# Second feed-forward product of a hybrid encoder block: block products of eight in place of plain products

## The chip, the cores and the metric

One Trainium2 chip, one of its cores. The metric is the device time of one execution of the whole program in microseconds (us). Engines are called PE (TensorE, matmuls), PEld (its weight loads), DVE (VectorE), ACT (ScalarE), POOL (GpSimd) and SP (SyncE, which here only starts DMA transfers).

## What is computed

The block takes x (1024 tokens of 1024 channels, float32) through a state-space branch, a sparse attention branch, a merge and a feed-forward part. Only the last part matters here:

```
h2 = rmsnorm(x, norm2_g)
g, up = split(h2 @ w_ffn_in, [2816])
x = x + (silu(g) * up) @ w_ffn_out
out = rmsnorm(x, norm_f_g)
```

`h2 @ w_ffn_in` is the first product (1024 channels in, 5632 out) and `(silu(g) * up) @ w_ffn_out` the second (2816 in, which is 22 tiles of 128, and 1024 out, which is 8 tiles of 128). All tensors lie transposed: channels on the 128 partitions, tokens along the free dimension, in halves H0 and H1 of 512.

## The kernel before, in words

**Precision.** Every operand is split into a high and a low part (`whi`, `wlo` for weights): ACT casts it to the matmul's format (`S.copy`, line 190, or line 88 in `load_w`), DVE subtracts the cast from the original (line 191, or 89). One product of a 128x128 weight tile with 512 tokens is then three matmuls: high by high, high by low, low by high.

**First product** (`ffn_pair`, lines 804 to 857, called 22 times at line 1040). One call makes one tile of `g` and one of `up` for all tokens. It treats them as a 2x2 block product and forms it, as Winograd's form of Strassen's scheme does, from seven block products in place of eight. A block product is 4 contraction tiles x 3 = 12 matmuls of 512 columns, so a call has 84. Four sums of weights (`s1` to `s4`) are formed on POOL (lines 811 to 814). The seven activation operands (`b11, t1, t2, b21, t3, b22, t4`) were formed earlier; each lies split in one of seven slots of 16 KB per partition (`mb0, mb1, ma0, ma1, c0, c1, c2`, given out by `slot`). Each block product has a PSUM bank of its own, taken in turn from `px` and `pg` (four banks each); DVE (line 836) and ACT (line 841) add the seven results to `gate` and `hid`. Then POOL multiplies `gate` by the row norm (line 853), ACT takes Silu (854), POOL multiplies again (855), DVE multiplies `hid` by it (856), and `hid` goes to a DRAM scratch `hscr` (857).

**Second product** (lines 1066 to 1095). The 22 contraction tiles are taken in stages of 8, 6, 4 and, as the tail, 4. `acts_in` (1041) reads `hscr` tile by tile, 512 KB each (line 1050), into a staging buffer (`hin`) and splits it into slots that are free again. Within a stage each of the 8 output tiles takes its weights by `load_w` and runs `fout` (859) on both halves: n contraction tiles x 3 matmuls into one bank, then one copy by ACT or one add by DVE into `x2[m]`. In the second stage the residual comes back from `x2scr` (`xin`, line 1086) and POOL adds it (1087).

**Tail** (lines 1114 to 1123). The last tiles run in token chunks of 512, 256 and 256. After each chunk the sum of squares is closed, the row norm is formed (`rstd_bcast`), and `finish` scales and writes the output.

**Staging buffers.** Two rotating buffers each lie under the names `eh` and `el` of pool `ep` (bufs=2, 4 KB per partition each). In the first product `gate` is an `eh` tile and `hid` an `el` tile; later `xin` takes `eh`, and the `hin` of the later stages take `el`. The first stage's `hin` use six buffers: two called `raw` and the four in which the weights `ra` and `rw` of the first product had been.

**Order of work.** The program is written engine by engine, and a scheduler in the compiler fixes the order of each engine's instructions beforehand; each engine and SP's queue then runs its list in order. A tile that finds no free buffer of its name waits until one is released.

Of the kernel before, what the change touches and what calls it, by code (L numbers as in the profile page):

```python
# [8 lines left out]
F32 = mybir.dt.float32  # L9
# [11 lines left out]
KT = 8  # L21
# [9 lines left out]
FT = FFN // P  # L31

# [8 lines left out]
AIN = 3  # L41
# [4 lines left out]
RAWT = None  # L46
# [11 lines left out]
def block_kernel(ctx, tc, xT, gv, wk, wfo, rope, s5s, s5b, s5c, ldt, dsk, cst, cm, out):  # L58
# [119 lines left out]
    hscr = dram.tile([FT, P, L], F32, name="hscr")  # L178
# [625 lines left out]
    def ffn_pair(j, B, ft, sm, first, hook=None):  # L804
        ra, rw = [wp.tile([P, KT, P], F32, tag="raw", name="raw") if first or t == RAWT else
                  ft.tile([P, KT, P], F32, tag=t, name=t, bufs=2) for t in ("ra", "rw")]
        SP.dma_start(out=ra, in_=wk[T_FFN + j])
        SP.dma_start(out=rw, in_=wk[T_FFN + FT + j])
        a11, a12, a21, a22 = ra[:, :4], ra[:, 4:], rw[:, :4], rw[:, 4:]
# [5 lines left out]
        state = {"n": 0}  # L815

        def mul(a, b):
            n = state["n"]
            if n % 2 == 0:
                state["w"] = (wp.tile([P, KT, P], F32R, tag="whi", name="whi"),  # L820
                              wp.tile([P, KT, P], F32R, tag="wlo", name="wlo"))
            state["n"] += 1
            hi, lo = [t[:, 4 * (n % 2):4 * (n % 2) + 4] for t in state["w"]]
            split(hi, lo, a)
            ps = (px, pg)[n % 2].tile([P, 512], F32, tag="xg"[n % 2], name="pm")
            for k in range(4):
                PE.matmul(ps, hi[:, k], b[:, k], start=(k == 0), stop=False)  # L827
                PE.matmul(ps, hi[:, k], b[:, 4 + k], start=False, stop=False)  # L828
                PE.matmul(ps, lo[:, k], b[:, k], start=False, stop=(k == 3))  # L829
            return ps  # L830

        def T(tag):
            return ft.tile([P, 512], F32, tag=tag, name=tag, bufs=2)

        def add(o, a, b):
            V.tensor_tensor(o, a, b, op=OP.add)  # L836
            return o
        gate = ep.tile([P, L], F32, tag="eh", name="gate")
        hid = ep.tile([P, L], F32, tag="el", name="hid")
        m1 = T("m1")  # L840
        S.copy(m1, mul(a11, B["b11"]))
        u2 = add(T("u2"), mul(s2, B["t2"]), m1)
        u3 = add(T("u3"), mul(s3, B["t3"]), u2)
        m5 = mul(s1, B["t1"])
        u4 = add(T("u4"), m5, u2)
        add(hid[:, H1], m5, u3)
        add(gate[:, H1], mul(s4, B["b22"]), u4)
        if hook:
            hook()
        add(gate[:, H0], mul(a12, B["b21"]), m1)  # L850
        add(hid[:, H0], mul(a22, B["t4"]), u3)
        for c in (H1, H0):
# [3 lines left out]
            V.tensor_tensor(hid[:, c], hid[:, c], gate[:, c], op=OP.mult)  # L856
        SP.dma_start(out=hscr[j], in_=hid)

    def fout(c, n, ws, acts, m, x2, first=False):
        hi, lo = ws  # L860
        ps = pg.tile([P, 512], F32, tag="g", name="g")[:, :c.stop - c.start]
        for k in range(n):
            PE.matmul(ps, hi[:, k], acts[k][0][:, c], start=(k == 0), stop=False)  # L863
            PE.matmul(ps, hi[:, k], acts[k][1][:, c], start=False, stop=False)  # L864
            PE.matmul(ps, lo[:, k], acts[k][0][:, c], start=False, stop=(k == n - 1))  # L865
        if first:
            S.copy(x2[m][:, c], ps)
        else:
            V.tensor_tensor(x2[m][:, c], ps, x2[m][:, c], op=OP.add)  # L869
# [137 lines left out]
    xg = xgp.tile([P, KT, L], F32, name="xg")  # L1007
    B = {"b22": slot("c0"), "t3": slot("c1"), "t2": slot("c2")}
# [29 lines left out]
    ft = tc.alloc_tile_pool(name="ft", bufs=1)  # L1038
    for j in range(FT):
        ffn_pair(j, B, ft, sm, j == 0, None if j else lambda: rstd_bcast(ep, ss, rb2, H0))  # L1040
    def acts_in(j0, n, keys, stage):
        r = []
        for q in range(n):
            if q % 2 == 0:
                t = slot(keys[q // 2])
            o = 4 * (q % 2)
            hi, lo = hl(t, o, 2), hl(t, o + 2, 2)
            pool, tag = stage[q % len(stage)]
            raw = pool.tile([P, KT, P], F32, tag=tag, name="hin", bufs=2).rearrange("p a b -> p (a b)")
            SP.dma_start(out=raw, in_=hscr[j0 + q])  # L1050
            split(hi, lo, raw)
            r.append((hi, lo))
        return r

    def tail_weights(k0, n, keys, r):
        for m in range(8):
            if m % 4 == 0:
                wt = slot(keys[m // 4])
            hi, lo = [wt[:, 2 * (m % 4) + q].rearrange("p (k d) -> p k d", k=4) for q in range(2)]
            raw = ep.tile([P, KT, P], F32, tag="el", name="raw")[:, :n]  # L1060
            SP.dma_start(out=raw, in_=wfo[m][:, k0:])
            split(hi, lo, raw)
            r.append((hi, lo))
            yield

    plan = ((8, ("mb0", "c2", "c1", "mb1")), (6, ("c0", "ma0", "ma1")), (4, ("mb0", "c2")), (4, ("c1", "mb1")))
    k0 = 0
    nxt = load_w(0, 8, wfo[0][:, :8])
    acts = acts_in(0, 8, plan[0][1], [(wp, "raw"), (ft, "ra"), (ft, "rw")])
    ft.release()  # L1070
    sm.release()
    xr = tc.alloc_tile_pool(name="xr", bufs=1)
    x2 = [xr.tile([P, L], F32, name=f"x2_{m}") for m in range(8)]
    for q, (n, _) in enumerate(plan[:-1]):
        n2, keys2 = plan[q + 1]
        for m in range(8):
            ws = nxt
            if m < 7:
                nxt = load_w(0, n, wfo[m + 1][:, k0:k0 + n])
            elif q < 2:  # L1080
                nxt = load_w(0, n2, wfo[0][:, k0 + n:k0 + n + n2])
            for c in HALVES:
                fout(c, n, ws, acts, m, x2, q == 0)
            if q == 1:
                t = ep.tile([P, L], F32, tag="eh", name="xin")
                SP.dma_start(out=t, in_=x2scr[m])
                G.tensor_tensor(x2[m], x2[m], t, op=OP.add)
            if m == AIN:
                acts2 = acts_in(k0 + n, n2, keys2, [(ep, "el")])
            if q == 2:  # L1090
                if m == 0:
                    wts = []
                    tw = tail_weights(k0 + n, n2, ("c0", "ma0"), wts)
                next(tw)
        acts = acts2
        k0 += n
    n = n2
    nt = [r32(slot("ma1")), r32(slot("mb0"))]
# [16 lines left out]
    for c in (H0, slice(512, 768), slice(768, 1024)):  # L1115
        for m in range(8):
            fout(c, n, wts[m], acts, m, x2)
            add_sq(x2[m][:, c], ss[:, c], m == 0)
            if m == 4 and last:
                finish(last)  # L1120
        rstd_bcast(ep, ss, rb2, c)
        last = c
# [85 lines left out]
```

## Time and profile before

| | us |
|---|---|
| three runs of the kernel | 1956.57 (median), 1956.02, 1960.09 |
| profiled execution, first to last instruction (its span) | 1953.5 |
| median less span, taken as what lies around the profiled span | 3.1 |
| first feed-forward product, from the trace | 1266.2 to 1692 |
| second product, stages of 8, 6 and 4 | 1692 to 1891 |
| tail, norm and output | 1891 to 1953.5 |

No time of its own is recorded for the profiled execution beside its span, so its own time is taken as span plus 3.1, which is the median.

How to read it: times of the trace count from the first instruction. PE's matmuls are pipelined, so a row shows 0.39 us for a matmul whose successor starts 0.23 us later; the pitch from start to start is what counts. "Idle before, releaser" names who ended a wait.

### The profile page before, as it was taken

How to read it: one execution, taken by the hardware profiler on the slowest of the kernel's cores; microseconds unless marked ns; L12 is line 12 of the kernel's file. 1: busy time of each engine (PE TensorE's matmuls, PEld its weight loads, DVE VectorE, ACT ScalarE, POOL GpSimd, SP SyncE). 2: the span in 40 equal slices, each digit the busy share in tenths (PEclk: the TensorE clock that was granted, in tenths of full speed). 3: DMA queues.
4: the chain of work that ended last, by engine and by line, in shares of the span. 5: the costliest groups of instructions: out<-in, count | busy, mean ns of one | idle time of the engine just before them, and what ended most of it. 6: DMA issues, size and time to landing. Idle time of an engine off the chain costs nothing.

```text
span 1953.5 us, 23933 instructions
## 1 busy us (share of the span) xinstructions
PE 1829.1 (94%) x8502; PEld 1510.8 (77%) x8502; DVE 1388.8 (71%) x2253; ACT 851.0 (44%) x1432; POOL 741.9 (38%) x512
## 2 busy tenths in 40 slices
PE   7999999996988888899999899999999999999997
PEld 6888777885766677777887678878888888788886
DVE  7966798779989878966568656786767666812355
ACT  5322245445455776145666744632332323422124
POOL 5168765446765321100000001356656566301303
PEclk9999999997999999999999999999999999999998
DMA  4553443422222332162237455432122221523322
GB/s 171 165 188 115 147 115 112 131 82 63 88 78 84 111 119 86 65 205 82 91 124 237 156 199 188 158 108 92 76 87 85 77 93 69 204 95 95 113 66 87
DMA packets 137447, 229.94 MB, mean 118 GB/s; under 512 B 26608, under 2 KB 78832, under 8 KB 137328
## 3 DMA queue, kind: packets, MB, share of 16 engines
q1 hardware_dynamic: 134704, 225.22, 35.1%
q10 hardware_dynamic: 2624, 3.20, 0.5%
q8 instruction: 67, 1.10, 0.2%
q14 instruction: 52, 0.43, 0.1%
HBM read 158.91 MB, written 66.06 MB: 115 GB/s over the span
## 4 chain that ended last, share of the span: by engine, by line
PE 55%; DVE 20%; ACT 6%; POOL 6%; DMA 6%; issue 5%; SPq 1%; DVEq 0%; ACTq 0%; POOLq 0%
PE pm L829 6%; PE pm L827 6%; PE pm L828 6%; PE g L865 4%; PE g L864 4%; PE g L863 4%; PE g L680 4%; PE g L681 4%; PE g L682 4%; DVE sc L358 2%; ACT junk L622 2%; PE g L208 2%; PE g L209 2%; PE g L207 2%; DVE wlo L89 2%
## 5 line engine op out<-in xcount | busy, mean ns | idle before, releaser
L209 PE MATMUL g<-h_hi,wlo 128*128 128x512 f32 (+1 forms) x704 | 277.2, 394 | 22.1 <-DVE wlo L89 22.1
L207 PE MATMUL g<-h_hi,whi 128*128 128x512 f32 (+1 forms) x704 | 276.8, 394 | 9.5 <-ACT whi L88 7.0
L208 PE MATMUL g<-h_lo,whi 128*128 128x512 f32 (+1 forms) x704 | 277.1, 394 | 2.1 <-DVE h_lo L156 2.1
L89 DVE TENSOR_TENSOR wlo<-raw,whi 128x1024 fp32r<-128x1024 f32 (+2 forms) x117 | 146.7, 1254 | 63.8 <-ACT whi L88 63.6
L209 PEld LDWEIGHTS g<-h_hi,wlo 128*128 128x128 f32 x704 | 135.4, 192 | 51.0 <-DVE wlo L89 25.8
L207 PEld LDWEIGHTS g<-h_hi,whi 128*128 128x128 f32 x704 | 135.4, 192 | 35.2 <-ACT whi L88 7.0
L88 ACT CAST whi<-raw 128x1024 fp32r<-128x1024 f32 (+2 forms) x89 | 88.4, 993 | 160.1 <-PE g L864 79.3
L208 PEld LDWEIGHTS g<-h_lo,whi 128*128 128x128 f32 x704 | 135.1, 192 | 29.2 <-DVE h_lo L156 3.5
L358 DVE SCALAR_TENSOR_TENSOR sc<-r,wq,sc 128x384 f32<-128x384 f32 (+3 forms) x160 | 148.7, 973 | 9.3 <-ACT r L357 8.4
L357 ACT ACTIVATE r<-ips,rqi 128x384 f32<-128x384 f32 (+3 forms) x160 | 93.8, 615 | 86.0 <-PE ips L356 47.0
L622 ACT ACTIVATE junk<-sc,nthr 128x384 bf16<-128x384 f32 (+1 forms) x124 | 96.3, 776 | 68.2 <-DVE nthr L618 66.0
L88 POOL CAST whi<-raw 128x1024 fp32r<-128x1024 f32 x28 | 33.9, 1212 | 220.2 <-PE g L681 105.6
L829 PE MATMUL pm<-c,wlo 128*128 128x512 f32 x264 | 103.7, 393 | 2.3 <-DVE wlo L191 2.3
L827 PE MATMUL pm<-c,whi 128*128 128x512 f32 x264 | 103.2, 391 | 0.0
L828 PE MATMUL pm<-c,whi 128*128 128x512 f32 x264 | 103.2, 391 | 0.0
L853 POOL TENSOR_TENSOR gate<-gate,rb 128x512 f32<-128x512 f32 x44 | 67.8, 1541 | 84.2 <-DVE gate L836 84.2
L1018 POOL TENSOR_TENSOR xg<-xg 128x512 f32<-128x512 f32 x4 | 7.1, 1779 | 240.7 <-ACT xg L791 240.7
L191 DVE TENSOR_TENSOR wlo<-s,whi 128x512 fp32r<-128x512 f32 x88 | 93.7, 1085 | 3.5 <-ACT whi L190 3.5
L856 DVE TENSOR_TENSOR hid<-hid,gate 128x512 f32<-128x512 f32 x44 | 53.1, 1209 | 47.4 <-POOL gate L855 47.4
L355 PE MATMUL ips<-ki,st 128*128 128x384 f32 (+3 forms) x160 | 64.9, 406 | 21.7 <-ACT r L357 17.1
L190 ACT CAST whi<-s 128x512 fp32r<-128x512 f32 x88 | 52.5, 621 | 64.8 <-PE pm L828 60.7
L869 DVE TENSOR_TENSOR x<-g,x 128x512 f32<-128x512 f32 (+1 forms) x56 | 34.1, 611 | 61.1 <-PE g L865 61.0
(388 smaller groups left out, 5278.3 us busy)
## 6 DMA issues: line engine op xcount, KB each, us to landing
raw<-in_wk SPq DMA_DIRECT2D x95, 512.0 KB, 4.2
hscr<-hid SPq DMA_DIRECT2D x22, 512.0 KB, 2.6
hin<-hscr SPq DMA_DIRECT2D x22, 512.0 KB, 3.8
ra<-in_wk SPq DMA_DIRECT2D x21, 512.0 KB, 3.2
rw<-in_wk SPq DMA_DIRECT2D x21, 512.0 KB, 3.2
gscr<-go SPq DMA_DIRECT2D x16, 512.0 KB, 4.9
q<-qscr SPq DMA_DIRECT2D x16, 512.0 KB, 4.9
st<-qiscr SPq DMA_DIRECT2D x16, 384.0 KB, 3.9
```

The source lines that it names most:

```text
L88: (eng or S.copy)(hi[:, :kt], raw[:, :kt])
L89: V.tensor_tensor(lo[:, :kt], raw[:, :kt], r32(hi[:, :kt]), op=OP.subtract)
L191: V.tensor_tensor(lo, src, r32(hi), op=OP.subtract)
L207: PE.matmul(ps, hi[:, k], act[0][:, k, c], start=(k == 0), stop=False)
L208: PE.matmul(ps, hi[:, k], act[1][:, k, c], start=False, stop=False)
L209: PE.matmul(ps, lo[:, k], act[0][:, k, c], start=False, stop=(k == KT - 1))
L357: S.activation(r, ps, AF.Relu, scale=rqi[:, i:i + 1])
L358: V.scalar_tensor_tensor(seg(i)[:, c], r, wq[:, i - 2, h:h + 1], seg(i)[:, c], op0=OP.mult, op1=OP.add)
L622: S.activation(junk2[:, :n], seg(j + 2), AF.Sign, bias=nthr.bitcast(F32)[:, j:j + 1], accum_out=cnt[:, j:j + 1])
L827: PE.matmul(ps, hi[:, k], b[:, k], start=(k == 0), stop=False)
L828: PE.matmul(ps, hi[:, k], b[:, 4 + k], start=False, stop=False)
L829: PE.matmul(ps, lo[:, k], b[:, k], start=False, stop=(k == 3))
```

## The change

**Second product.** 16 of the 22 contraction tiles (`WK = 16`) are taken as two groups (g = 0, 1) of eight. A group is a block product of 4 pairs of contraction tiles with 4 pairs of output tiles (q = 0 to 3), each in seven block products of 12 matmuls (`out_pair`, through the new `winograd`). The last 6 tiles make up the tail, which keeps its three chunks.

**Activations.** The seven operands of a group are formed on DVE in `ffn_pair` from two neighbouring `hid` tiles (four subtractions per two calls) and written to a DRAM scratch `tscr`, 256 KB each, seven per two calls, in place of `hscr`. `refill` brings one operand back into the slot of the same name: two reads of 512 KB into `eh` buffers, each split by ACT and DVE. It is called as soon as the previous user's block product of that name has been written: in the last call of `ffn_pair` for group 0, in the last `out_pair` of group 0 for group 1. In the last `out_pair` of group 1 `tail_fill` loads the tail's operands and weights instead.

**Weights.** `out_raw` loads two output tiles' weights of 8 contraction tiles; POOL forms the four sums, ACT and DVE split seven half tiles, as in the first product.

**Block sums.** In both products four of the seven block products accumulate in one bank (A) one after another, two in a bank B, one alone. ACT or DVE reads the sum out of bank A between two of them. The first product's DVE adds out of PSUM fall from seven to three per call (its last product is multiplied straight out of PSUM), its ACT copies rise from one to three. The order of the seven is now `b11, t1, t2, b21, t3, b22, t4`.

```
+    def winograd(a, B, sm, sink, after=None):
...
+        plan = ((a11, "b11", "A", "m1"), (s1, "t1", "B", "m5"), (s2, "t2", "A", "u2"), (a12, "b21", "D", "d"),
+                (s3, "t3", "A", "u3"), (s4, "b22", "B", "e"), (a22, "t4", "A", "c21"))
...
             for k in range(4):
-                PE.matmul(ps, hi[:, k], b[:, k], start=(k == 0), stop=False)
...
+                PE.matmul(ps, hi[:, k], b[:, k], start=(fresh and k == 0), stop=False, skip_group_check=True)
...
+            sink(stage, ps)
+            if after:
+                after(n, key)
...
+            if stage in ("m1", "m5", "u2"):
+                S.copy({"m1": m1, "m5": m5, "u2": u2}[stage], ps)
...
+            elif stage == "u3":
+                V.tensor_tensor(hid[:, H1], ps, m5, op=OP.add)
...
+            sub(t3, hid[:, H1], h[:, H1])
+            sub(h[:, H1], h[:, H1], h[:, H0])
+            sub(t2, hid[:, H1], h[:, H1])
+            sub(t4, hid[:, H0], t2)
...
+    def refill(key, g):
+
+        t = slot(SLOT[key])
+        for h in range(2):
+            raw = ep.tile([P, L], F32, tag="eh", name="hin")
+            SP.dma_start(out=raw.rearrange("p (k c) -> p k c", k=2),
+                         in_=tscr[ORDER.index(key), 4 * g + 2 * h:4 * g + 2 * h + 2].rearrange("k p c -> p k c"))
+            hi, lo = hl(t, 2 * h, 2), hl(t, 4 + 2 * h, 2)
+            split(hi, lo, raw)
+        return t
...
+    def out_pair(g, q, a, B, sm, x2, after=None):
...
+            if g == 0 and stage in ("m1", "m5", "u2", "c21"):
+                S.copy(x, ps)
+            else:
+                V.tensor_tensor(x, ps, x, op=OP.add)
...
-    plan = ((8, ("mb0", "c2", "c1", "mb1")), (6, ("c0", "ma0", "ma1")), (4, ("mb0", "c2")), (4, ("c1", "mb1")))
...
+    for g in range(N_G):
+        B, refilled = refilled, {}
+        for q in range(4):
+            a, after = nxt, None
+            if (g, q) != (N_G - 1, 3):
+                nxt = out_raw(g + (q == 3), (q + 1) % 4)
+            if q == 3:
+                after = (lambda i, key: refilled.update({key: refill(key, g + 1)})) if g < N_G - 1 else tail_fill
+            out_pair(g, q, a, B, sm, x2, after)
+            if g == 0:
+                for m in (2 * q, 2 * q + 1):
+                    t = ep.tile([P, L], F32, tag="eh", name="xin")
+                    SP.dma_start(out=t, in_=x2scr[m])
+                    G.tensor_tensor(x2[m], x2[m], t, op=OP.add)
```

## Rows read from the trace of the kernel before

**Rows 1.** The page, busy time and share of the span of each engine.
```profile
PE 1829.1 (94%) x8502; PEld 1510.8 (77%) x8502; DVE 1388.8 (71%) x2253; ACT 851.0 (44%) x1432; POOL 741.9 (38%) x512
```

**Rows 2.** Stretches: length, PE, PEld, DVE, ACT, POOL busy, clock, DMA share, GB/s.
```profile
1380.00:1420.00 40.00, 40.00 (x178) 33.15 (x177) 27.73 (x34) 11.41 (x20) 23.39 (x16) 1.00 0.23 85
...
1692.00:1720.00 28.00, 25.09 (x110) 20.44 (x110) 17.84 (x16) 12.65 (x16) 6.63 (x3) 1.00 0.66 226
```

**Rows 3.** Longest wait of PE from 1240 on: for whom, us, times, longest.
```profile
PE g L865 <- DVE wlo L89: 2.6, 1, 2.6
```

**Rows 4.** Timeline of PE: start, duration; one block product, then matmuls of 256 columns.
```profile
1266.20 0.39 PE L827 MATMUL pm<-mb,whi 128*128 128x512 f32 x1
...
1268.92 0.39 PE L827 MATMUL pm<-c,whi 128*128 128x512 f32 x1
...
1924.23 0.28 PE L864 MATMUL g<-mb,ma 128*128 128x256 f32 x1
...
1925.43 0.28 PE L865 MATMUL g<-c,ma 128*128 128x256 f32 x1
```

**Rows 5.** The tile hin: ns min/median/max of cast and subtraction; landing of the read.
```profile
L190 ACT CAST c<-hin x10: 1052/1055/1062, 1679.6 to 1855.3; 128x1024 fp32r<-128x1024 f32 x10
L191 DVE TENSOR_TENSOR c<-hin,c x10: 1207/1222/2326, 1681.9 to 1856.4; 128x1024 fp32r<-128x1024 f32 x10
...
DMA to landing us min/median/max: 3.1/3.8/6.7
```

**Rows 6.** Timeline of SP: when reads of hscr were issued, stages one and two.
```profile
1693.92 0.32 SPq L1050 DMA_DIRECT2D hin<-hscr  x1
...
1701.80 0.51 SPq L1050 DMA_DIRECT2D hin<-hscr  x1
...
1709.49 0.32 SPq L1050 DMA_DIRECT2D hin<-hscr  x1
...
1712.03 0.32 SPq L1050 DMA_DIRECT2D hin<-hscr  x1
...
1715.18 0.32 SPq L1050 DMA_DIRECT2D hin<-hscr  x1
...
1719.12 0.32 SPq L1050 DMA_DIRECT2D hin<-hscr  x1
```

**Rows 7.** Timeline: last uses of two gate tiles (DVE) and first issues of xin (SP).
```profile
1670.31 0.69 DVE L836 TENSOR_TENSOR gate<-pm,m 128x512 f32<-128x512 f32 x1 [2.03 <-PE pm L829]
...
1676.93 0.68 DVE L856 TENSOR_TENSOR hid<-hid,gate 128x512 f32<-128x512 f32 x1
...
1685.33 0.42 SPq L1086 DMA_DIRECT2D xin<-x2scr  x1
...
1698.85 1.78 DVE L856 TENSOR_TENSOR hid<-hid,gate 128x512 f32<-128x512 f32 x2
...
1701.08 0.38 SPq L1086 DMA_DIRECT2D xin<-x2scr  x1
```

**Rows 8.** The tile xin: POOL's add, ns min/median/max.
```profile
L1087 POOL TENSOR_TENSOR x<-x,xin x8: 2769/3088/3089, 1791.6 to 1848.7; 128x1024 f32<-128x1024 f32 x8
```

**Rows 9.** PE behind a wait (timeline), and the stretch that follows (columns as above).
```profile
1302.15 0.79 PE L829 MATMUL pm<-c,wlo 128*128 128x512 f32 x1 [2.25 <-DVE wlo L191]
...
1302.74:1305.30 2.56, 2.56 (x7) 1.97 (x6) 2.56 (x4) 0.00 (x0) 0.77 (x1) 0.50 0.39 110
```

**Rows 10.** Reading a bank in the first product: ACT's copy, DVE's add; splits on DVE.
```profile
L841 ACT COPY m<-pm x22: 572/590/590, 1279.3 to 1676.2; 128x512 f32<-128x512 f32 x22
...
L836 DVE TENSOR_TENSOR hid<-pm,u x44: 673/678/692, 1281.9 to 1698.3; 128x512 f32<-128x512 f32 x44
...
L191 DVE TENSOR_TENSOR wlo<-s,whi x88: 674/1146/1781, 1267.0 to 1680.7; 128x512 fp32r<-128x512 f32 x88
```

**Rows 11.** A stretch with three transfers under way, columns as in the second group.
```profile
1700.00:1704.00 4.00, 4.00 (x19) 3.30 (x18) 2.90 (x4) 1.25 (x2) 0.00 (x0) 1.00 0.91 311
```

More of the change, by code (lines that the diff above doesn't have):

```diff
@@ L40 @@
 SSV = 5
-AIN = 3
 GPW = 4
@@ L802, in hl @@
         return t[:, k] if n == 1 else t[:, k:k + n].rearrange("p a b -> p (a b)")
[L804 to L809, printed above, removed]
+    ORDER = ("b11", "t1", "t2", "b21", "t3", "b22", "t4")
+    def winograd(a, B, sm, sink, after=None):
+        a11, a12, a21, a22 = a
         s1, s2, s3, s4 = [sm.tile([P, 4, P], F32, tag=f"s{q}", name=f"s{q}") for q in range(1, 5)]
@@ L832, in T @@
[L832 to L837, printed above, removed]
+                pair = (wp.tile([P, KT, P], F32R, tag="whi", name="whi"),
+                        wp.tile([P, KT, P], F32R, tag="wlo", name="wlo"))
+            hi, lo = [t[:, 4 * (n % 2):4 * (n % 2) + 4] for t in pair]
+            split(hi, lo, w)
+            fresh = bk not in bank
+            if fresh:
+                bank[bk] = (pg if bk == "A" else px).tile([P, 512], F32, tag="g" if bk == "A" else "x", name="pm")
@@ new lines, in winograd, with ffn_pair @@
+            ps, b = bank[bk], B[key]
+            for k in range(4):
+                PE.matmul(ps, hi[:, k], b[:, k], start=(fresh and k == 0), stop=False, skip_group_check=True)
+                PE.matmul(ps, hi[:, k], b[:, 4 + k], start=False, stop=False, skip_group_check=True)
+                PE.matmul(ps, lo[:, k], b[:, k], start=False, stop=(k == 3), skip_group_check=True)
+            sink(stage, ps)
+            if after:
+                after(n, key)
+    def ffn_pair(j, B, ft, sm, held, hook=None, after=None):
+        ra, rw = [wp.tile([P, KT, P], F32, tag="raw", name="raw") if j == 0 else
+                  ft.tile([P, KT, P], F32, tag=t, name=t, bufs=2) for t in ("ra", "rw")]
+        SP.dma_start(out=ra, in_=wk[T_FFN + j])
+        SP.dma_start(out=rw, in_=wk[T_FFN + FT + j])
@@ L851, in ffn_pair, with act @@
-        add(hid[:, H0], mul(a22, B["t4"]), u3)
-        for c in (H1, H0):
+        m1, m5, u2 = [ft.tile([P, 512], F32, tag=t, name=t) for t in ("m1", "m5", "u2")]
+        def act(c):
             G.tensor_tensor(gate[:, c], gate[:, c], rb2[:, c], op=OP.mult)
@@ L860, in fout @@
         hi, lo = ws
-        ps = pg.tile([P, 512], F32, tag="g", name="g")[:, :c.stop - c.start]
+        w = c.stop - c.start
+        o = c.start % 512
+        ps = pg.tile([P, 512], F32, tag="g", name="g")[:, :w]
         for k in range(n):
[L863 to L869, printed above, removed]
+            xh, xl = acts[c.start // 512][k]
+            PE.matmul(ps, hi[:, k], xh[:, o:o + w], start=(k == 0), stop=False)
+            PE.matmul(ps, hi[:, k], xl[:, o:o + w], start=False, stop=False)
+            PE.matmul(ps, lo[:, k], xh[:, o:o + w], start=False, stop=(k == n - 1))
@@ L1038, in block_kernel @@
     ft = tc.alloc_tile_pool(name="ft", bufs=1)
+    held = []
+    N_G = WK // 8
+    refilled = {}
     for j in range(FT):
[L1040 to L1053, printed above, removed]
@@ L1067, in block_kernel @@
-    k0 = 0
-    nxt = load_w(0, 8, wfo[0][:, :8])
-    acts = acts_in(0, 8, plan[0][1], [(wp, "raw"), (ft, "ra"), (ft, "rw")])
+        last = j == FT - 1
+        ffn_pair(j, B, ft, sm, held, None if j else lambda: rstd_bcast(ep, ss, rb2, H0),
+                 (lambda n, key: refilled.update({key: refill(key, 0)})) if last else None)
     ft.release()
-    sm.release()
     xr = tc.alloc_tile_pool(name="xr", bufs=1)
     x2 = [xr.tile([P, L], F32, name=f"x2_{m}") for m in range(8)]
[L1074 to L1096, printed above, removed]
@@ L1100, in finish @@
+    nt = [r32(slot(SLOT["t4"])), None]
     def finish(c):
```

119 lines of the change are left out of this document (79 added, 40 removed).

## The prediction

> **What bounds the kernel now.** I read the page first: PE is busy for 94% of the span, no other engine for over 71% [rows 1]. Then the stretches: in the first feed-forward product PE is busy for 40.0 of 40 us at full clock while DVE has 12 us to spare; the place where PE loses most is the handover from the first product to the second, 25.1 busy of 28 us [rows 2]. Then PE's waits: from 1240 on the longest is 2.6 us, at that same handover, for a weight split on DVE [rows 3]. So PE's work sets the time here, and whatever makes PE wait at a handover is added to it. The base of the sum is the profiled execution: span 1953.5 plus 3.1 around it, the median 1956.6.
>
> **What PE is spared.** Twelve matmuls of 512 columns, one block product, take 1268.92 - 1266.20 = 2.72 us, 0.2267 each; ten steps of 256 columns take 1.20 us, 0.120 each [rows 4]. Before: 18 contraction tiles x 8 output tiles x 2 halves x 3 = 864 matmuls of 512, in the tail 4 x 8 x 3 = 96 of 512 and 192 of 256. After: 8 calls x 84 = 672, in the tail 6 x 8 x 3 = 144 of 512 and 288 of 256. That is 144 fewer of 512, 32.6 us, and 96 more of 256, 11.5 us: **-21.1 us**, all on the path. The wait of 2.6 us at the old handover goes with the code that caused it [rows 3]: **-2.6**. What is late next is counted under the two refills.
>
> **Inside the calls.** A call lasts 7 x 2.72 = 19.0 us. In the first product DVE loses four adds of 0.68 per call and gains two subtractions on average, ACT gains two copies of 0.59 [rows 10]; both have the room [rows 2]. `out_pair` has the same splits and POOL sums as `ffn_pair` and fewer steps behind them, so its cover is the same. The new wait is the read of bank A: PE may not add to it before ACT or DVE has read it. One other block product, 2.72 us, lies between; the last matmul's tail (0.39 - 0.23) and a copy or add of 0.59 to 0.68 leave 1.8 us. A weight split ahead of the read on DVE lasts 1.15 at the median, 1.78 at most [rows 10]: 0 taken, bound 0.7 us a set when it fails. Behind a late read on DVE stand the next splits, for which PE waits next. The seven `tscr` writes per two calls come behind SP's wait for DVE; `ra` and `rw` for the call after next queue there with one call, 19 us, to spare: 0.
>
> **The two refills.** This is the unknown. Before a group's first `out_pair`, seven slots must be filled anew: 14 reads of 512 KB through the two `eh` buffers, each held through landing, cast and subtraction. By medians that is 3.8 + 1.06 + 1.22 = **6.1 us a turn** [rows 5]. Turns of the same kind, two buffers of `el` in rotation, show it whole: issued 1709.49, next issue in that buffer 1715.18, a turn of 5.7; 1712.03 to 1719.12, 7.1; and with one buffer, at the handover, 1693.92 to 1701.80, 7.9 [rows 6]. I take 6.1, between the first two, and keep 5.7 and 7.9 as ends. A buffer is not taken ahead of the tiles whose first write stands earlier in the program: `xin`'s source was written before the first product began, but its first two reads left at 1685.33 and 1701.08, behind the last uses of the last two gates (ended 1677.6 and 1700.6) [rows 7].
>
> First refill, t from the start of the last `ffn_pair`. Uninterrupted, that call and the first `out_pair` would end at 38.1. The call before releases its gate 4.6 after its end: the last gate add, 1670.31, starts as that block product ends, one block product (2.72) before the call's end, and the last use ends at 1677.6, 7.3 after the add [rows 7]; the change leaves that position as it is. Half operand 1 sits in a free buffer before t = 0 and is split behind the first block product, done at 5.0; half 2 goes at 4.6, done at 10.7; halves 3 to 5 at 11.1, 16.8, 17.2. Now this call's own gate, first written after its fourth block product, takes a buffer, until 17.2 + 7.3 = 24.5. Half 6 at 22.9, then both buffers: 7 and 8 at 29.0 and 30.6, and so on by 6.1 to 47.3 and 48.9 for 13 and 14. The last block product still needs 1.4: 50.3, **12.2 late**. (Turn 5.7: 9.8; 7.9: 23.2.)
>
> Second refill, t from the last `out_pair` of group 0. The two `xin` of the pair before hold the buffers until POOL has added them, 3.09 each [rows 8]: the first until about 1.2 (its sums close a block product earlier), the second until 4.2. Seven turns each end at 4.2 + 42.7 = 46.9, plus 1.4, against 38.1: **10.2 late**. (Turn 5.7: 7.4; 7.9: 22.8.)
>
> While PE waits for the seventh operand it can run up to two block products of the next pair, since the weight buffers hold two pairs of splits: up to 5 us each time, 4 taken: -8. Behind a wait PE restarts slowly: after 2.25 us idle the granted clock was 0.50, the 1.2 GHz level, and six matmuls took 2.56 us, 0.43 each in place of 0.23: 1.2 us, with the one ahead of them some 1.5 us lost [rows 9]. The wait of 2.6 [rows 3] was at full clock throughout [rows 2], so I count one in two: **+1.5**.
>
> The tail's own fill needs no turn of that length: its slots come free from the second block product on, and its weights are used one output tile every 18 x 0.2267 = 4.1 us. Taken as 0; bounds -1.5 (more room for the norm in the longer chunks) and +3.
>
> Sum: -21.1 - 2.6 + (12.2 + 10.2 - 8) + 1.5 = -7.8: **1948.8 us**. With 5.7 it is 1943.6; by the same steps 6.4 gives 14.0 and 12.3 late and 1952.7. The gain is gone at a turn of about 6.7.
>
> The page "DMA: Bandwidth & Descriptors" of the Trainium skill (Anatomy of one DMA) gives a transfer about 2.0 us plus its bytes over 436 GB/s, fitted on transfers issued by GpSimd; for 512 KB that is an estimate of 3.2 us. The trace has 3.1 at the least and 3.8 at the median [rows 5], so the measurement is used. With 3.2 the turn would be 5.5 and the sum about 1941.
>
> **The rivals.**
> *Refills hidden.* If a stage's reads overlap as freely as their bytes allow, 14 x 0.524 MB at the 311 GB/s seen with three transfers under way [rows 11] take 23.6 us, less than the 33 us between the first free slot and the last need. Then only -21.1 - 2.6 remain: 1932.9. Against it: two buffers cannot hold three reads, and no row shows a turn under 5.7 [rows 6]. The same page's Specifications put the ceiling of the 16 engines at 435 GB/s, an estimate of 16.9 us for these bytes.
> *Slower: the `eh` buffers at the crowded handover.* DVE subtracts refills between splits, sums and gates there, and with POOL active a subtraction has lasted 2.33 in place of 1.22 [rows 5]; the turn seen in that place is 7.9 [rows 6]. Then 23.2 + 22.8 - 8 = 38.0 late: 1972.4. It decides from 6.7 on. For it: in the crowded stretch the one-buffer turn. Against: once PE waits, splits and sums come less often.
> *Slower: bank A.* If the read misses its 1.8 us by 0.7 in each of the 30 sets, 21 us are added: about 1970. Against: DVE is idle 30% of this stage, and the order is made beforehand.
> *No change.* A turn of 6.4 to 7.0, refills eating what the block products save: 1953 to 1960.
> That fewer matmuls are issued than counted, or more, is no rival: the counts follow from the loops.
>
> **How the numbers follow.** About 0.2%, 3.9 us, is what a measurement of this kernel can tell from no change. Forecast (turn 5.7 to 6.4, 1943 to 1952.7): 0.34. Refills hidden wholly or mostly: 0.16. No change: 0.22. Slow turn: 0.20; bank A: 0.08. So faster 0.50, same 0.22, slower 0.28. The predicted time is the forecast's, 1949. The range of 8 in 10 runs from the hidden refills, 1933, to the slow turn, 1972; the likeliest case's own range is 1943 to 1953.
>
> **What would show it.** Right: PE at full pitch in both products, 84 matmuls per call, and two stretches in which PE waits for the subtraction into a slot, block product by block product, the last operands latest; two reads into `eh` outstanding at most, turns of 5.7 to 7.1. Wrong: no such wait (hidden refills, 1933); waits of PE for ACT or DVE reading the accumulating bank in every call; a tail that starts late for its operands; a `gate` that waits for a buffer so long that the last first-product call itself is stretched.

## The result and the profile after

The changed kernel takes 1987.8 us (median of four runs, 1986.9 to 1990.9) against 1956.3 (1954.5 to 1960.1) for the kernel before, run beside it: a ratio of 1.0154, 95% interval 1.0135 to 1.0173. That is 31.5 us slower, where 7.8 us faster was forecast, and outside the range. The profiled execution has a span of 1986.8 us, 33.3 more than before.

The page of the changed kernel, busy time and instructions of each engine, answers to [rows 1]:

```profile
PE 1831.8 (92%) x8454; PEld 1501.2 (76%) x8454; DVE 1363.7 (69%) x2251; ACT 896.2 (45%) x1522; POOL 780.8 (39%) x544
```

PE has 48 matmuls fewer, as counted: 144 of 512 columns less, 96 of 256 more. Still its busy time is 2.7 us longer than before, part of it being at a lower clock, and its idle time rose by the other 30.6 us. Where, the stretches tell (changed kernel; length, then PE, PEld, DVE, ACT, POOL busy, clock, DMA share, GB/s, as in [rows 2]):

```profile
1380.00:1420.00 40.00, 38.66 (x170) 31.34 (x169) 21.38 (x28) 13.29 (x24) 22.63 (x17) 1.00 0.27 99
1700.00:1720.00 20.00, 18.61 (x82) 14.76 (x81) 13.44 (x14) 12.77 (x18) 8.34 (x6) 1.00 0.46 166
1720.00:1740.00 20.00, 13.59 (x45) 9.26 (x44) 13.28 (x13) 7.40 (x11) 7.15 (x5) 0.76 0.58 190
1740.00:1760.00 20.00, 18.32 (x63) 13.18 (x63) 12.46 (x12) 8.61 (x13) 8.97 (x5) 0.81 0.61 204
1760.00:1780.00 20.00, 19.52 (x86) 15.85 (x85) 8.06 (x12) 6.66 (x12) 14.09 (x9) 1.00 0.41 136
1800.00:1820.00 20.00, 14.82 (x56) 11.72 (x55) 10.90 (x14) 8.33 (x10) 5.12 (x3) 0.83 0.57 194
1820.00:1840.00 20.00, 16.75 (x71) 12.65 (x69) 14.34 (x17) 9.24 (x12) 4.56 (x3) 1.00 0.66 213
1840.00:1860.00 20.00, 18.40 (x78) 14.33 (x79) 13.93 (x15) 5.25 (x9) 10.77 (x6) 1.00 0.50 160
```

Three losses are to be seen. **Every call of the first product** loses: 170 matmuls in the first of these stretches, where the kernel before has 178 in the same one [rows 2]. **Every set of the second product** loses likewise (1760 to 1780: 86, where full pitch shows 90). And the **two handovers** lose 258 - 190 = 68 and 258 - 205 = 53 matmuls in 60 us each against the pace of 86, (68 + 53) x 0.2267 = 27 us.

How long a call is, ACT's copy of the first block product shows (timeline of ACT, changed kernel; the copies of the neighbouring calls):

```profile
1440.08 0.59 ACT L854 COPY m<-pm 128x512 f32<-128x512 f32 x1 [1.80 <-PE pm L833]
...
1460.09 0.59 ACT L854 COPY m<-pm 128x512 f32<-128x512 f32 x1 [1.80 <-PE pm L833]
...
1480.11 0.59 ACT L854 COPY m<-pm 128x512 f32<-128x512 f32 x1 [1.80 <-PE pm L833]
```

A call lasts 20.01 us; before it was 19.04. The copy of the last call starts at 1700.27 in place of 1676.20: 24.1 us lost by then. Of these, 19.5 come from the last twenty calls, 0.97 each, and 4.6 from the first two, where PE waits once for ACT's copy of the first sum out of bank A, which stands behind the splits that close the stage before. PE's waits in 1240 to 1340, then in 1340 to 1660 (for whom, us, times and the longest):

```profile
PE pm L831 <- ACT m L854: 3.8, 1, 3.8
```

```profile
PE pm L831 <- ACT whi L190: 10.7, 16, 0.7
```

The timeline of all engines around the end of one call (rows of PEld left out) shows the place:

```profile
1471.35 1.29 POOL L848 TENSOR_TENSOR gate<-gate,rb 128x512 f32<-128x512 f32 x1 [1.26 <-DVE gate L863]
...
1472.67 0.63 ACT L849 ACTIVATE gate<-gate 128x512 f32<-128x512 f32 x1 [3.48 <-POOL gate L848]
1472.81 0.39 PE L833 MATMUL pm<-c,wlo 128*128 128x512 f32 x1
1473.21 0.60 ACT L190 CAST whi<-ra 128x512 fp32r<-128x512 f32 x1
1473.23 0.69 DVE L861 TENSOR_TENSOR hid<-pm,m 128x512 f32<-128x512 f32 x1 [1.96 <-PE pm L833]
...
1473.87 0.50 PE L831 MATMUL pm<-mb,whi 128*128 128x512 f32 x1 [0.67 <-ACT whi L190]
1474.20 0.40 PE L832 MATMUL pm<-mb,whi 128*128 128x512 f32 x1
1474.43 0.40 PE L831 MATMUL pm<-ma,whi 128*128 128x512 f32 x1
```

The matmul at 1472.81 is the last of t3, into bank A; DVE's read of hid out of bank A (L861) follows; then come two matmuls of the next call's b11 (mb) and at 1474.43 the first of t4 (ma), again into bank A. The program has b22 between t3 and t4. PE's instruction list as compiled has not: there the order is b11, t1, b21, t2, b22, t3, two matmuls of the next b11, t4. And those two wait 0.67 us for their cast on ACT.

Three causes can be read into these rows. **A**, the bank: t4 may not start before DVE has read bank A, which ends at 1473.92, and PE's list has next to nothing to do meanwhile. **B**, the list of ACT: the cast of b11's weights stands behind a Silu that waits for POOL. **C**, the weight buffers: that cast goes into the buffer that t3's last matmuls release, so it cannot start earlier anyway. The cast ends at 1473.81 and DVE's read at 1473.92, so these rows alone do not tell which of them holds PE. A fourth lies outside: the operands' subtractions and writes that were added. The experiments take these in turn, and then the handovers.

### The profile page after: what moved, and what is told of

Read it like the earlier page. It is cut to its first block, busy times and chain, and to the rows that moved or that the text cites. A ratio compares the mean times of both kernels' runs of the same rounds, so it can differ in the third digit from the quotient of the medians.

```text
span 1986.8 us, 24088 instructions
## 1 busy us (share of the span) xinstructions
PE 1831.8 (92%) x8454; PEld 1501.2 (76%) x8454; DVE 1363.7 (69%) x2251; ACT 896.2 (45%) x1522; POOL 780.8 (39%) x544
## 4 chain that ended last, share of the span: by engine, by line
PE 53%; DVE 21%; DMA 7%; ACT 7%; POOL 5%; issue 5%; SPq 1%; ACTq 0%; DVEq 0%; POOLq 0%
PE pm L831 9%; PE pm L832 9%; PE pm L833 8%; PE g L680 4%; PE g L681 3%; PE g L682 3%; DVE sc L358 2%; ACT junk L622 2%; PE g L208 2%; PE g L209 2%; PE g L207 2%; DVE wlo L88 2%; DMA hin<-tscr 2%; DVE a L569 1%; DMA gate<-gscr 1%
## 5 line engine op out<-in xcount | busy, mean ns | idle before, releaser
L832 PE MATMUL pm<-c,whi 128*128 128x512 f32 x360 | 143.1, 398 | 5.0 <-DVE c L191 5.0
L831 PE MATMUL pm<-c,whi 128*128 128x512 f32 x360 | 143.0, 397 | 4.9 <-ACT m L854 3.8
L833 PE MATMUL pm<-c,wlo 128*128 128x512 f32 x360 | 142.7, 396 | 1.3 <-DVE wlo L191 1.3
L88 DVE TENSOR_TENSOR wlo<-raw,whi 128x1024 fp32r<-128x1024 f32 x93 | 123.0, 1323 | 15.4 <-ACT whi L87 15.1
L191 DVE TENSOR_TENSOR wlo<-s,whi 128x512 fp32r<-128x512 f32 x120 | 88.0, 754 | 53.8 <-ACT whi L190 53.6
L190 ACT CAST whi<-s 128x512 fp32r<-128x512 f32 x120 | 71.4, 619 | 116.3 <-PE pm L832 95.5
L831 PE MATMUL pm<-mb,whi 128*128 128x512 f32 x240 | 97.1, 405 | 22.0 <-ACT whi L190 21.9
L87 ACT CAST whi<-raw 128x1024 fp32r<-128x1024 f32 x65 | 68.1, 1048 | 75.8 <-PE g L681 22.1
L1077 POOL TENSOR_TENSOR xg<-xg 128x512 f32<-128x512 f32 x4 | 7.1, 1780 | 241.0 <-ACT xg L791 241.0
L831 PE MATMUL pm<-ma,whi 128*128 128x512 f32 x240 | 95.6, 398 | 4.7 <-ACT ma L190 4.1
L832 PE MATMUL pm<-ma,whi 128*128 128x512 f32 x240 | 95.0, 396 | 1.2 <-DVE ma L191 1.2
L833 PE MATMUL pm<-ma,wlo 128*128 128x512 f32 x240 | 94.5, 394 | 0.0
```

Source lines behind the costliest of these rows:

```text
L87: (eng or S.copy)(hi[:, :kt], raw[:, :kt])
L88: V.tensor_tensor(lo[:, :kt], raw[:, :kt], r32(hi[:, :kt]), op=OP.subtract)
L191: V.tensor_tensor(lo, src, r32(hi), op=OP.subtract)
L831: PE.matmul(ps, hi[:, k], b[:, k], start=(fresh and k == 0), stop=False, skip_group_check=True)
L833: PE.matmul(ps, lo[:, k], b[:, k], start=False, stop=(k == 3), skip_group_check=True)
```

## The experiments

In each diff the line with "-" is the changed kernel's. "Matmuls" are the numbers in a stretch, as above.

### Is it the first product, and the accumulation?

**Seven banks again in the first product, the rest as changed.** The body of `ffn_pair` is the old one, products in the order b11, t2, t3, t1, b22, b21, t4, with DVE's seven adds.

```
-        winograd((ra[:, :4], ra[:, 4:], rw[:, :4], rw[:, 4:]), B, sm, sink, after)
+            ps = (px, pg)[n % 2].tile([P, 512], F32, tag="xg"[n % 2], name="pm")
...
+        u2 = add(T("u2"), mul(s2, "t2"), m1)
+        u3 = add(T("u3"), mul(s3, "t3"), u2)
```

> The first product goes back to seven PSUM banks per call with its sums on DVE; the writes of the operands, the refills and the second product stay as in the changed kernel. In the changed kernel a call lasts 20.02 us in place of 19.03, and PE waits 0.67 us once in each call, behind the product t3 and ahead of t4. Theory (all its forms: the wait lies inside the calls of the first product and comes from the accumulation): a call lasts 19.03 to 19.1 again, 22 x 1.0 = 22 us less, about 1966. Rival (the calls are longer because of the operands' subtractions on DVE and their writes, which stay here): about 1988.

Measured: 1976.3 us, ratio to before 1.0095 (1.0080 to 1.0110). The first copies of the calls follow one another by 19.04 and 19.73 in turn; the last one starts at 1683.28, 17.0 us earlier than in the changed kernel. Most of the loss in the calls is the accumulation's. Two things were not expected: every second call, as long as operands are formed, keeps a wait for a low part of weights on DVE, and of the 17.0 us only 11.5 arrive at the end. The handover takes back the rest (1700 to 1720: 27 matmuls).

**The first product alone changed, second as before.**

```
-        if j >= WK:
-            SP.dma_start(out=hscr[j - WK], in_=hid)
...
+        SP.dma_start(out=hscr[j], in_=hid)
```

> The kernel before with the first product alone changed: sums by accumulation, order b11, t1, t2, b21, t3, b22, t4; hid is written as before and the second product is the old one. Theory: 22 calls x 1.0 us = 22 us slower than before, about 1978, with the 0.67 us wait of PE in every call. Rival (operands' subtractions and writes): about 1956, calls of 19.03.

Measured: 1982.3 us, 1.0120 (1.0103 to 1.0137), 24.9 more than the kernel before beside it. Its calls last 20.04 us with the same wait, 10.7 us in 16 calls of the stretch 1340 to 1660, exactly as in the changed kernel. Neither the subtractions nor the second product is needed for it.

### Which wait?

**Silu no longer behind POOL.**

```
-                act(H1)
+                V.tensor_tensor(gate[:, H1], gate[:, H1], rb2[:, H1], op=OP.mult)
+                S.activation(gate[:, H1], gate[:, H1], AF.Silu)
+                G.tensor_tensor(gate[:, H1], gate[:, H1], rb2[:, H1], op=OP.mult)
```

> The changed kernel with one step moved: the first multiplication of the second half of gate by the row norm runs on DVE (0.7 us) in place of POOL (1.29 us), so that Silu, behind which the cast of the next call's b11 weights stands on ACT, no longer waits for POOL. The order of every engine's list of PE and ACT is otherwise the same. Theory B (that Silu holds the cast back, and the cast holds PE): the wait goes, calls of 19.1, about 1967. Theory A with C (bank A holds t4 until DVE has read it, and the cast can start only when t3 has freed its weight buffer): the cast starts at most 0.25 us earlier, calls of 19.8, 1982 to 1985.

Measured: 1983.2 us, 1.0139 (1.0122 to 1.0156); a call lasts 19.86. PE's waits in 1340 to 1660:

```profile
PE pm L831 <- ACT whi L190: 8.4, 16, 0.5
```

It was 10.7, 16, 0.7. B adds 0.15 us to a call and is not the cause.

**A third buffer for the high parts of the weights.**

```
-                pair = (wp.tile([P, KT, P], F32R, tag="whi", name="whi"),
+                rot[0] += 1
+                pair = ((w3 if w3 and rot[0] % 3 == 0 else wp).tile([P, KT, P], F32R, tag="whi", name="whi"),
```

> In the first product alone the high parts of the weights have three buffers in rotation in place of two; banks as in the changed kernel. PE's list then has the first matmuls of the next call ahead of t3, and t4 directly behind t3 with nothing between. Theory A (reading bank A): PE waits for DVE's read of hid between t3 and t4, 0.7 to 0.95 us in each call, and the calls stay at 19.8 to 20.1: 1983 to 1990. Theory C (weight buffer) and theory B (the cast stands behind a Silu that waits for POOL): no wait is left, calls of 19.1, about 1966.

Measured: 1984.4 us, 1.0134 (1.0119 to 1.0149); a call lasts 20.07 us, averaged from the first copy to the last. PE's waits in 1340 to 1660, then its timeline at the end of a call:

```profile
PE pm L832 <- DVE hid L862: 12.5, 16, 0.8
```

```profile
1471.66 0.39 PE L834 MATMUL pm<-c,wlo 128*128 128x512 f32 x1
1472.83 0.50 PE L832 MATMUL pm<-ma,whi 128*128 128x512 f32 x1 [0.78 <-DVE hid L862]
1473.17 0.40 PE L833 MATMUL pm<-ma,whi 128*128 128x512 f32 x1
```

The cast is early now and b11's first matmuls stand ahead of t3; t4 follows t3 with nothing between, and PE waits for DVE's read of the bank. From start to start the step takes 1.17 us in place of 0.23, and the next one 0.34: together 1.05, a call's whole loss. B and C are out of the way here and the loss is the same, so A alone is enough to make it. In the changed kernel the waits for A and for C end some 0.1 us apart, and taking away C alone gives nothing back. DVE's read wants the sum without t4, so t4 has to come after it. The page "PSUM — Partial Sum Buffer" of the Trainium skill (Terms, PSUM bank) states that PE's write and DVE's or ACT's access to one bank at the same time is an error. The trace agrees: t4 starts 0.05 us after the end of DVE's read, at 1472.78.

**t4 in a bank of its own.**

```
-                (s3, "t3", "A", "u3"), (s4, "b22", "B", "e"), (a22, "t4", "A", "c21"))
+                (s3, "t3", "A", "u3"), (s4, "b22", "B", "e"), (a22, "t4", own, "c21"))
...
+                S.copy(u3, ps)
+                V.tensor_tensor(hid[:, H1], u3, m5, op=OP.add)
...
+                V.tensor_tensor(hid[:, H0], ps, u3, op=OP.add)
```

> In the first product alone the last product t4 gets a bank of its own; ACT copies the sum of t3 out (one copy of 0.59 more per call) and DVE adds it (one add of 0.68 more). PE's list then has t4 ahead of t3 or shared around it, and next call's b11 after both. Theory A (t4 may not start before DVE has read bank A behind t3, 0.9 us after t3's last matmul, and only two matmuls fill that): no wait is left, calls of 19.0 to 19.1, about 1966. Theory C (the split weights of the next call's b11 go into the buffer that t3 gives free last, so that their cast of 0.6 us starts only when t3 has ended): where b11 still follows t3 directly, every second call, a wait of 0.5 to 0.7 us stays, about 1976.

Measured: 1981.7 us, 1.0116 (1.0100 to 1.0131). Two calls last 38.9 us, 19.46 each. PE's waits in 1340 to 1660:

```profile
PE pm L833 <- DVE wlo L191: 4.2, 8, 0.6
```

Neither the bank nor the cast (C) is waited for any more; what stays is, every second call, a low part of weights on DVE. The last copy starts 11.7 us earlier, and only 6.1 arrive at the end.

**The same work in another order.** No instruction is added or taken away; only the order in the program changes, and with it PE's list, which now has ten matmuls or more between any two products into bank A. The new list also puts other products between t3 and the next call's b11, as the run before does, so these two runs take away A and C together; the run with the third buffer is the one that parts them.

```
-        plan = ((a11, "b11", "A", "m1"), (s1, "t1", "B", "m5"), (s2, "t2", "A", "u2"), (a12, "b21", "D", "d"),
-                (s3, "t3", "A", "u3"), (s4, "b22", "B", "e"), (a22, "t4", "A", "c21"))
+        plan = ((a11, "b11", "A", "m1"), (s2, "t2", "A", "u2"), (s1, "t1", "B", "m5"), (s4, "b22", "B", "e"),
+                (s3, "t3", "A", "u3"), (a12, "b21", "D", "d"), (a22, "t4", "A", "c21"))
```

> The changed kernel with one edit: the seven block products of a set stand in the program as b11, t2, t1, b22, t3, b21, t4 in place of b11, t1, t2, b21, t3, b22, t4. Work, banks, buffers and instructions are the same; in PE's list there are then ten or more matmuls between any two products into bank A, where the changed kernel has two between t3 and t4. Theory A (bank A): no wait of PE inside the calls, 19.03 to 19.1 us each in the first product and about 19.1 in the second, 22 + 6 us spared, of which the handover may take back some, as in the run with t4 in a bank of its own (12 us spared in the calls, 6 to 8 in all): 1958 to 1972. Theories B and C (Silu, weight buffers), as the sums and splits have the same resources: 1980 to 1988.

Measured: 1978.7 us, 1.0112 (1.0094 to 1.0130). PE's waits in 1240 to 1700:

```profile
PE pm L830 <- ACT m L853: 6.7, 1, 6.7
PE pm L832 <- DVE wlo L191: 3.4, 8, 0.7
```

The wait of every call is gone, as A has it; the time lies between the two ranges, for three reasons that the stretches show (same columns as above):

```profile
1266.00:1300.00 34.00, 27.29 (x115) 21.93 (x114) 21.10 (x33) 14.91 (x26) 15.05 (x11) 0.85 0.30 103
1380.00:1420.00 40.00, 39.62 (x174) 32.28 (x173) 23.31 (x30) 13.72 (x24) 24.72 (x18) 1.00 0.27 99
1620.00:1660.00 40.00, 40.00 (x178) 33.12 (x178) 20.09 (x26) 15.36 (x27) 23.95 (x17) 1.00 0.21 79
1700.00:1720.00 20.00, 16.92 (x65) 13.01 (x65) 16.82 (x15) 9.23 (x14) 8.01 (x5) 0.91 0.39 137
1720.00:1740.00 20.00, 13.02 (x39) 8.39 (x38) 10.26 (x10) 7.90 (x10) 6.83 (x4) 0.83 0.74 255
```

The very first call now waits 6.7 us for ACT's copy out of bank A, which stands behind the splits that close the stage before (115 matmuls; the changed kernel has 126, the kernel before 154). As long as operands are formed PE gets 174 matmuls in 40 us, in the last six calls, which form none, 178: DVE's queue does cost something. And the last copy starts at 1691.19, 9.1 us earlier than in the changed kernel, while the median time is 9.1 us shorter too (6.6 in the profiled execution), though the sets of the second product no longer wait either: the handovers took those 6 us back.

### The handovers

**Four staging buffers for the refills.**

```
-            raw = ep.tile([P, L], F32, tag="eh", name="hin")
+            raw = ep.tile([P, L], F32, tag=("eh", "el")[h], name="hin")
```

> The changed kernel with its refills staged through four buffers (eh and el in turn) in place of the two of eh. In the changed kernel the halves follow one another by 3.3 to 3.8 us, a turn of 6.6 to 7.6 in two buffers, and PE loses some 13 to 17 us at each handover. Theory (the turn through two buffers sets the handover): halves follow one another by about 2 us until the block products that free the slots set the pace; 10 to 18 us less, 1970 to 1978. Rival (casts of refills stand on ACT ahead of the casts that the current calls need, and SP starts the reads in program order, so the pace is that of the lists): 1984 to 1990.

Measured: 1974.6 us, 1.0090 (1.0075 to 1.0105), 13.3 less than the changed kernel. The stretches of this run:

```profile
1700.00:1720.00 20.00, 16.24 (x69) 12.74 (x68) 17.61 (x16) 13.21 (x18) 11.31 (x7) 0.93 0.55 186
1720.00:1740.00 20.00, 19.95 (x79) 15.97 (x78) 15.18 (x18) 10.68 (x15) 2.74 (x2) 0.89 0.84 296
1740.00:1760.00 20.00, 18.63 (x78) 14.26 (x78) 12.70 (x10) 6.04 (x11) 16.53 (x11) 1.00 0.40 129
1800.00:1820.00 20.00, 15.88 (x63) 12.36 (x62) 17.45 (x18) 12.96 (x16) 2.98 (x1) 0.91 0.84 286
```

With 1820 to 1860 (79 and 87) the two handovers now lose 32 and 29 matmuls in place of 68 and 53: 13.6 us, which is what the time shows. The two buffers' turn was a bound, and half of the loss; the other half stays, with DMA engines and DVE both nearly full in these stretches.

The rival holds in part too. In the changed kernel's second handover PE's longest wait is not for a refill but for a cast of weights. ACT runs its list in order, and that cast stands behind a refill's cast, which waits for its read (ACT, then PE, changed kernel):

```profile
1812.67 1.04 ACT L190 CAST c<-hin 128x1024 fp32r<-128x1024 f32 x1 [3.21 <-DMA hin<-tscr]
1813.62 0.61 ACT L190 CAST whi<-raw 128x512 fp32r<-128x512 f32 x1
```

```profile
1814.29 0.79 PE L831 MATMUL pm<-mb,whi 128*128 128x512 f32 x1 [5.18 <-ACT whi L190]
```

Those weights had landed by 1788.5, and the operand was ready at 1804.7. With four buffers the same wait is still 4.12 us long. No run puts these casts in another order, so what that would give is not shown.

**Both edits.** New order and four buffers.

> Both edits together, the order b11, t2, t1, b22, t3, b21, t4 and four staging buffers for the refills. If the two theories hold and add up: 28 us less in the calls and 10 to 18 at the handovers, 1942 to 1952, faster than the kernel before. If the handover takes back what the calls spare: 1958 to 1970.

Measured: 1965.9 us, 1.0046 (1.0031 to 1.0061). The two gains add up (9.1 + 13.3 = 22.4; measured 21.9), but the first had been overestimated.

### How far it can be repaired

**Three edits more:** seven banks for the first call alone, the residual added in group 1, and `ra` and `rw` as further staging buffers of the first refill.

```
+        if j == 0:
+            first_call(ra, rw, B, ft, sm, gate, hid, hook)
...
-            if g == 0:
+            if g == N_G - 1:
...
+        tag = ("ra", "rw", "eh", "el")[nref[0] % 4]
```

> The run with the new order and four staging buffers, and three edits more, each of which acts in a stretch of its own: the first call of the first product uses seven banks again (there PE waited 6.7 us for ACT's copy out of bank A, behind the splits that close the stage before; 1266 to 1340 should come back from 290 matmuls to some 310, 4 to 5 us); the residual is added in group 1 in place of group 0, so that its reads leave the eh buffers to the second refill; the first refill also uses the four buffers of the weights ra and rw. Theory (staging buffers bound the handovers): each handover loses 3 to 6 us less, in all 1950 to 1957. Rival (DMA at 0.84 to 0.86 busy, 286 to 296 GB/s, and the ACT list bound them already): only the 4 to 5 us at the start, 1960 to 1963.

Measured: 1958.2 us, 1.0006 (0.9995 to 1.0017): as fast as the kernel before, and between the two ranges. The start came back as expected (1266 to 1340: some 310 matmuls). At the first handover the bound moved once more. The run's stretch:

```profile
1700.00:1720.00 20.00, 12.74 (x47) 9.77 (x48) 18.25 (x18) 10.27 (x14) 4.73 (x3) 0.91 0.56 183
```

DVE is busy 18.25 of 20 us and DMA 0.56: with the buffers there, refill subtractions, splits and sums queue on DVE. PE's waits in this stretch agree: 3.0 us for a low part of weights and 2.8 for the read of a bank, both on DVE, and 1.9 for a cast on ACT.

**Two of the four operand subtractions on POOL.**

```
-            sub(t3, hid[:, H1], h[:, H1])
+            sub(t3, hid[:, H1], h[:, H1], G)
...
-            sub(t4, hid[:, H0], t2)
+            sub(t4, hid[:, H0], t2, G)
```

> As the run before, and two of the four subtractions per two calls that form the operands of the second product go from DVE to POOL. In the runs with the new order PE was busy 39.62 of 40 us in calls that form operands and 40.00 in the last six, which form none, the difference being waits for low parts of weights on DVE. Theory (DVE's queue, which I had counted as having room): 40.00 throughout, 4 to 5 us less than the run before. Rival (POOL's sums for the next call come late instead): the same or slower.

Measured: 1959.6 us, 1.0001 (0.9992 to 1.0011). PE is busy 39.43 of 40 us, not 40.00: the theory fell. The trace shows why. In all seven waits of 1340 to 1660 the low part that PE waits for stands on DVE right behind one of the two operand subtractions left there, and that one takes 1.67 us beside POOL where the other takes 0.68 (DVE, then PE):

```profile
1393.14 0.68 DVE L927 TENSOR_TENSOR hid<-hid 128x512 f32<-128x512 f32 x1
1393.85 1.67 DVE L927 TENSOR_TENSOR t<-hid 128x512 f32<-128x512 f32 x1
1395.45 1.28 DVE L191 TENSOR_TENSOR wlo<-s,whi 128x512 fp32r<-128x512 f32 x2
```

```profile
1396.18 0.50 PE L832 MATMUL pm<-mb,wlo 128*128 128x512 f32 x1 [0.58 <-DVE wlo L191]
```

**Seven banks in every call, with the new staging.**

```
+        u2 = add(T("u2"), mul(s2, "t2"), m1)
+        u3 = add(T("u3"), mul(s3, "t3"), u2)
...
+            raw = stage(g, h)
...
-            if g == 0:
+            if g == N_G - 1:
```

> The kernel with seven banks in every call of the first product, its first order and DVE's sums (the first experiment, 1976), with the second product and the buffers of the run with all edits: block products with order b11, b22 and so on as there are, four staging buffers and those of ra and rw, residual in group 1. Second product still by accumulation in the changed kernel's order. If accumulation in the first product gives nothing where PE is the bound: within 6 us of the run with all edits. If the DVE time it saves matters at the handover: 8 us and more behind it.

Measured: 1960.2 us, 1.0021 (1.0011 to 1.0031), 2 us from the run with all edits. The two runs differ in one thing more: the sets of the second product still have the changed kernel's order here, and its wait (86 matmuls in 20 us). In 1380 to 1420, inside the first product, PE gets 175 matmuls against 174. Where PE sets the time, DVE adds that the accumulation spares are worth next to nothing.

**Every third refill subtraction on POOL.**

```
-            split(hi, lo, raw)
+            S.copy(hi, raw)
+            (G if nref[0] % 3 == 0 else V).tensor_tensor(lo, raw, r32(hi), op=OP.subtract)
```

> The run with all edits and sums of the second product's operands on DVE (1958, as fast as the kernel before), with every third of the refills' subtractions on POOL in place of DVE. In that run DVE worked without a gap from 1693 to 1718, at the first handover, and PE got 47 matmuls of 90 into 1700 to 1720; PE lost some 9 us at each handover. Theory (with the buffers there, DVE's subtractions bound the handover): nine subtractions of 1.2 us leave DVE, 3 to 6 us less, 1951 to 1955. Rival (POOL's subtraction takes over 2.5 us and lengthens those of DVE beside it, as its adds do): 1956 to 1962.

Measured: 1965.6 us, 1.0042 (1.0027 to 1.0058), a miss beyond the rival's range. Timelines of POOL and DVE in this run:

```profile
1709.74 2.79 POOL L956 TENSOR_TENSOR c<-hin,c 128x1024 fp32r<-128x1024 f32 x1
```

```profile
1710.26 3.35 DVE L956 TENSOR_TENSOR c<-hin,c 128x1024 fp32r<-128x1024 f32 x1
...
1715.80 1.21 DVE L956 TENSOR_TENSOR ma<-hin,ma 128x1024 fp32r<-128x1024 f32 x1
```

Beside POOL's subtraction of 2.8 us the same one on DVE takes 3.35 in place of 1.21. What was taken from DVE came back as slower DVE work: in 1700 to 1720 DVE is busy 19.93 us, where it was 18.25, and PE gets 37 matmuls in place of 47. No version tried is faster than the kernel before.

## Why the prediction was wrong

**What PE is spared**: the count was right (48 matmuls fewer by number); the old handover wait is gone. No run measures the 21.1 us by itself, but the sum below closes with it.

**Inside the calls** is the step that failed: "its cover is the same" and "One other block product, 2.72 us, lies between ... 0 taken". It lies between in the program, not in PE's list, where b21 and b22 had moved ahead of the products that wait for bank A, and t3 and t4 met. The price is 0.97 us a call, and with the wait for ACT's copy in the first call 24.1 us by the last call of the first product; in the second product it is 0.78 a set, some 6 us in eight sets. I had this as the rival "bank A", with 0.7 us a set and 21 us in all, and gave it 0.08, because DVE was idle 30% of the time and the order is made beforehand. That its time of about 1970 lies nearer to the result is in part luck: its mechanism was a read that comes late on DVE, and the read was not late. The two reasons for the 0.08 are true and neither is evidence: DVE's read started 0.4 us after t3's last matmul, without any delay, and the order made beforehand was the trouble.

**"Both have the room"**: nearly. DVE's operand subtractions cost about 0.9 us in every two calls once nothing hides them (174 for 178 matmuls in 40 us, some 6 to 7 us in the kernel).

**The two refills**: mechanism right, size off. The turn of 6.1 us in two buffers was too short. ACT's and DVE's timelines of the changed kernel, casts of the seventh, the ninth and the last half operand of the first refill, and the ninth and the last subtraction, and the landing of `hin` (its least value is a read of 256 KB in the tail), answer to [rows 5, 6]:

```profile
1725.49 1.05 ACT L190 CAST ma<-hin 128x1024 fp32r<-128x1024 f32 x1 [3.63 <-DMA hin<-tscr]
...
1733.45 1.05 ACT L190 CAST c<-hin 128x1024 fp32r<-128x1024 f32 x1 [0.99 <-DMA hin<-tscr]
...
1751.92 1.05 ACT L190 CAST ma<-hin 128x1024 fp32r<-128x1024 f32 x1 [1.24 <-DMA hin<-tscr]
```

```profile
1736.43 1.86 DVE L191 TENSOR_TENSOR c<-hin,c 128x1024 fp32r<-128x1024 f32 x1
...
1753.01 2.02 DVE L191 TENSOR_TENSOR ma<-hin,ma 128x1024 fp32r<-128x1024 f32 x1 [0.43 <-ACT ma L190]
```

```profile
DMA to landing us min/median/max: 2.6/3.8/6.5
```

From the seventh to the last, seven halves take 26.4 us: 3.8 each, a turn of 7.6. In the second refill the casts run from 1802.37 to 1842.00, twelve steps of 3.3, a turn of 6.6. By medians the landing is as before, and casts and subtractions too; the turn is not made of medians. From the eighth half to the last of the first refill three things add up: reads that land up to 5.6 us after their issue (together 3.9 us over the median; DMA engines are 0.89 busy from 1726 to 1731), subtractions that wait behind other work in DVE's list (3.0), and subtractions that last up to 2.3 us (2.8). The casts do not wait in ACT's list there: each starts 0.02 us after its read has landed. The last operand was ready at 1755.0, where 1694 + 48.9 = 1742.9 had been worked out. Some 4 of these 12 us stood already at the first half, done 9.1 us after the start of the last call and not 5.0: PE's list has t4 of the call before inside b11, so b11's slot comes free later. There too the program's order had been taken for PE's list.

The clock was taken too lightly as well: 1.5 us for both handovers. In the changed kernel the granted clock was 0.50 for some 17 us of the first and some 7 of the second. How much of that the waits for operands would have covered, no run shows. The stretch in the first (columns as in [rows 2]):

```profile
1731.00:1747.00 16.00, 11.39 (x24) 7.40 (x24) 9.77 (x7) 6.26 (x7) 7.31 (x4) 0.50 0.67 222
```

In all, the handovers lose 27.4 us in place of 12.2 + 10.2 - 8 + 1.5 = 15.9.

**The sum**: -7.8 + 24.1 + 6 + 11.5 = 33.8, where 11.5 is 27.4 - 15.9; the spans differ by 33.3. The tail, taken as 0, needs no term.

**The rival "refills hidden"** fails also with four buffers: DMA engines are then 0.84 busy at 286 to 296 GB/s and half of the loss stays.

## What to carry to other kernels

An accumulation that is read on its way ties two products to one bank; whether other work lies between them is to be read from the engine's instruction list as the compiler made it, not from the program, and a mere reordering of the program can restore it. Price a mechanism by what happens when it strikes in every iteration, and check that in the list before giving it a small chance. Where several resources stand behind one another (staging buffers, DMA, a vector engine's queue), a gain upstream is given back at the next one, so add up what arrives at the end and not what is spared on the way. In a list that runs in order, a cast that waits for a read holds up every cast behind it, also those whose data are there.

## What the runs showed of the hardware that I had not expected

Short stops are cheap to restart: after 0.78 us of waiting in each call (the run with a third buffer) the matmuls started 0.34, then 0.23 us apart, with a granted clock of 1.00 in 1380 to 1420. Longer ones are not all alike. The wait of 2.6 us in the kernel before stayed at 1.00 [rows 2, 3], the one of 2.25 us was followed by 0.50 [rows 9]. In the changed kernel's first handover PE was busy 2.22 of 5 us from 1726 to 1731, with waits of 0.3, 0.8 and 2.7 us, and from 1731 to 1747 the clock was 0.50, the 1.2 GHz level: 24 matmuls in 11.39 busy us. What decides between these cases, no run here parts.

DVE's subtraction of 1024 columns went from 1.21 to 3.35 us beside a subtraction on POOL, more than the 2.33 of [rows 5]. In the run with every third refill subtraction on POOL, the ten that DVE made with no POOL instruction beside them lasted 1.21 to 1.23 us each; the longest of those beside one lasted 3.42.
